# The down projection of a SwiGLU block: 16 of 22 inner tiles as a 2x2 block product with seven half products

## The chip, the cores and the metric

The kernel runs on one core of a Trainium2 chip. The core has five engines that work side by side, each through its own queue in order: TensorE (PE, matrix products; its weight loads are listed as PEld), VectorE (DVE), ScalarE (ACT), GpSimd (POOL) and SyncE (SP, which issues the transfers here). They meet at semaphores. Matrix products go to PSUM, eight banks of 128 x 512 float32; all else lies in SBUF. The metric is the device time of one execution in microseconds, the median of several.

## The reference

A trunk of two layers over 512 tokens with 1024 channels. Each layer is FFN, mixer, FFN, each between two RMS norms:

```python
def swiglu_ffn(h, w_gate, w_up, w_down):
    return (jax.nn.silu(h @ w_gate) * (h @ w_up)) @ w_down

def reference(x, ...):
    for l in range(DEPTH):
        h = rms_norm(x, norm_pre[l, 0])
        x = x + 0.5 * rms_norm(swiglu_ffn(h, ffn1_w_gate[l], ...), norm_post[l, 0])
        h = rms_norm(x, norm_pre[l, 1])
        x = x + rms_norm(hybrid_mixer(h, ...), norm_post[l, 1])
        h = rms_norm(x, norm_pre[l, 2])
        x = x + 0.5 * rms_norm(swiglu_ffn(h, ffn2_w_gate[l], ...), norm_post[l, 2])
    return x
```

The inner width of an FFN is 2816, which is 22 tiles of 128. So there are four FFNs, and in each a down projection: 512 tokens x 2816 by 2816 x 1024. The mixer (attention, convolution, gated linear attention) is not touched.

## The kernel before

**Precision.** Every float32 operand is split into a high part, which ScalarE casts to the type `float32r`, and a low part, which VectorE makes as operand minus high part (`split`, lines 107 and 108). A product is three matmuls: high by high, high by low, low by high. All matmuls are issued by `mm` (line 66).

**Gate and up.** `block_tiles` computes inner tiles 3 to 21 as 2x2 block products in seven half products each ("product" g; 12 matmuls of 256 columns). Weights are loaded raw, summed and split six products ahead of use; the split normalised input stands in `xh` and `xl` (128 x 8 x 512). Of every product ScalarE or VectorE takes results from PSUM (`cp`), and the tile's hidden values land in `hid[f]` (128 inner x 512 tokens), with f from 0 to 21. `between(g)` lets other work into that loop.

**Down.** `out_proj` has eight banks `o`: four token groups i of 128 times two column halves h of 512. For each inner tile k it loads 128 x 1024 weights (512 KB), splits them (`whi`, `wlo`) and the hidden tile (`sh`, `sl`), and issues 8 x 3 matmuls of 512 columns, hidden tile stationary and weights moving. The last four tiles (`TAIL`) go token group by token group, so that `finish(i)` (post norm, residual, next pre norm) of a finished group runs beside the matmuls of the next one. `early` loads the first weights of the next block.

**What sets the order.** A tile framework allocates buffers from pools in turn and puts in the waits; what passes through `pinned` or `mm` keeps the order in which it is written, other instructions can be moved ahead within their engine. Pool `wp` has five buffers for `whi`, five for `wlo`, and three for `raw`, each with room for two loads of 512 KB: a `raw` buffer is free when both its loads are used. Pool `tp` has slots of 128 x 512, 16 under tag "t", 14 under "s", 10 under "q". In the profile `whi<-raw` is the cast of weights and `wlo<-raw,whi` their low part, `sh<-hid` and `sl<-hid,sh` the same of a hidden tile.

## Time and profile before

| | |
|---|---|
| Median of 3 runs (lowest to highest) | 2366.95 us (2366.07 to 2367.29) |
| The profiled execution, its time and its span | 2367.24 us, 2365.5 us |
| TensorE busy | 2347.7 us, 99%, at the full clock |
| VectorE, ScalarE, GpSimd busy | 1629.1, 1117.9, 181.1 us |
| Down projections of the four FFNs, first `o` matmul at | 244.0, 1066.7, 1416.7, 2239.4 us |
| Transfers | 231.74 MB, mean 98 GB/s |

How to read it: a matmul's duration overlaps with the next one's, so what a matmul takes of TensorE is the distance from its start to the next start. The same holds, more weakly, on the other engines: an instruction's duration includes a tail under which the next one on the engine already begins; a consumer on another engine waits for the end. The busy share is an average over stages that differ widely.

### The profile page before, as it was taken

What the parts mean: (1) busy time and instruction counts of PE and PEld (TensorE: products, weight loads), DVE (VectorE), ACT (ScalarE), POOL (GpSimd) and SP (SyncE); (2) the same over time, 40 slices, a digit from 0 to 9 for tenths busy, and PEclk for the clock granted to TensorE, in tenths of its full rate; (3) what the DMA queues carried; (4) which work ended last, traced back from release to release, by engine and by line L of the source; (5) the groups of instructions that cost most, each with busy time, mean ns of one, the idle gap of its engine ahead of it and who ended that gap; (6) DMA issues with size and microseconds to landing.
All of it is one profiled execution on the core that took longest, in us unless ns stands there. A gap on an engine that the chain in (4) does not pass through costs nothing. (4 is left out here: it accounts for less than half of the span.)

```text
span 2365.5 us, 35797 instructions
## 1 busy us (share of the span) xinstructions
PE 2347.7 (99%) x14264; PEld 2094.3 (89%) x14264; DVE 1629.1 (69%) x2329; ACT 1117.9 (47%) x2148; POOL 181.1 (8%) x287
## 2 busy tenths in 40 slices
PE   8999999999999999999999999999999999999998
PEld 7999888887888899998899998888878888999987
DVE  7888436859965388884388883478599644888833
ACT  5556325644323365563356562356333333555622
POOL 0000001201011100000000000012010211000000
PEclk9999999999999999999999999999999999999999
DMA  5333323231333223333233343241313332333430
GB/s 171 96 102 107 142 89 103 69 94 54 108 90 107 81 72 108 108 110 141 71 87 102 100 133 116 73 116 55 110 54 106 91 95 75 90 108 108 134 107 36
DMA packets 307159, 231.74 MB, mean 98 GB/s; under 512 B 11722, under 2 KB 284140, under 8 KB 306992
## 3 DMA queue, kind: packets, MB, share of 16 engines
q1 hardware_dynamic: 306992, 229.46, 32.5%
q8 instruction: 111, 1.82, 0.3%
q14 instruction: 56, 0.46, 0.1%
HBM read 227.32 MB, written 2.10 MB: 97 GB/s over the span
## 5 line engine op out<-in xcount | busy, mean ns | idle before, releaser
L108 DVE TENSOR_TENSOR wlo<-raw,whi 128x1024 fp32r<-128x1024 f32 (+1 forms) x266 | 330.4, 1249 | 224.5 <-ACT whi L107 217.6
L107 ACT CAST whi<-raw 128x1024 fp32r<-128x1024 f32 (+1 forms) x266 | 278.1, 1046 | 399.3 <-PE gate L66 131.3
L336 DVE TENSOR_TENSOR wlo<-raw,whi 128x1024 fp32r<-128x1024 f32 (+1 forms) x304 | 331.1, 1089 | 125.0 <-ACT whi L334 124.8
L334 ACT CAST whi<-raw 128x512 fp32r<-128x512 f32 x532 | 315.1, 619 | 154.0 <-DVE raw L336 154.0
L66 PE MATMUL o<-whi,sh 128*128 128x512 f32 x704 | 274.2, 389 | 0.0
L66 PE MATMUL o<-wlo,sh 128*128 128x512 f32 x704 | 273.9, 389 | 0.0
L66 PE MATMUL o<-whi,sl 128*128 128x512 f32 x704 | 273.9, 389 | 0.0
L336 DVE TENSOR_TENSOR raw<-raw 128x512 f32<-128x512 f32 x304 | 209.3, 688 | 6.4
L108 DVE TENSOR_TENSOR sl<-hid,sh 128x512 fp32r<-128x512 f32 x88 | 60.0, 689 | 190.9 <-ACT sh L107 190.9
L66 PE MATMUL A<-xh,wlo 128*128 128x256 f32 x608 | 172.1, 283 | 0.0
L66 PE MATMUL A<-xl,whi 128*128 128x256 f32 x608 | 172.1, 283 | 0.0
L66 PE MATMUL A<-xh,whi 128*128 128x256 f32 x608 | 172.0, 283 | 0.0
L706 DVE SCALAR_TENSOR_TENSOR y<-u,cw,y 128x511 f32<-128x511 f32 (+14 forms) x240 | 166.7, 755 | 0.0
L107 ACT CAST sh<-hid 128x512 fp32r<-128x512 f32 x88 | 54.4, 622 | 230.5 <-PE o L66 230.5
L66 PEld LDWEIGHTS o<-whi,sl 128*128 128x128 f32 x704 | 132.1, 188 | 27.4
L66 PEld LDWEIGHTS o<-whi,sh 128*128 128x128 f32 x704 | 132.2, 188 | 27.3
L66 PEld LDWEIGHTS o<-wlo,sh 128*128 128x128 f32 x704 | 132.2, 188 | 27.2
L66 PE MATMUL gate<-xh,whi 128*128 128x512 f32 x384 | 151.3, 394 | 0.0
L66 PE MATMUL gate<-xh,wlo 128*128 128x512 f32 x384 | 149.8, 390 | 1.3 <-DVE wlo L108 1.3
L66 PE MATMUL gate<-xl,whi 128*128 128x512 f32 x384 | 149.6, 390 | 0.0
L195 POOL TENSOR_TENSOR rs<-ms,mhalf 128x1 f32<-128x1 f32 x48 | 30.9, 644 | 1454.4 <-DVE ms L193 1454.4
L66 PEld LDWEIGHTS A<-xh,whi 128*128 128x128 f32 x608 | 116.7, 192 | 0.2
(278 smaller groups left out, 6227.1 us busy)
## 6 DMA issues: line engine op xcount, KB each, us to landing
raw<-in_w_in_dram SPq DMA_DIRECT2D x108, 512.0 KB, 4.8
raw<-in_ffn_w_down_dram SPq DMA_DIRECT2D x88, 512.0 KB, 4.4
raw<-in_ffn_w_gate_dram SPq DMA_DIRECT2D x152, 256.0 KB, 3.3
raw<-in_ffn_w_up_dram SPq DMA_DIRECT2D x152, 256.0 KB, 4.6
raw<-in_w_branch_dram SPq DMA_DIRECT2D x24, 512.0 KB, 3.7
raw<-in_w_out_dram SPq DMA_DIRECT2D x16, 512.0 KB, 4.4
raw<-in_ffn_w_gate_dram SPq DMA_DIRECT2D x12, 512.0 KB, 4.8
raw<-in_ffn_w_up_dram SPq DMA_DIRECT2D x12, 512.0 KB, 4.6
```

The lines of the kernel that those rows point to most:

```text
L66: tc.keep_in_program_order(nc.tensor.matmul(*a, **k))
L107: nc.scalar.copy(hi, src)
L108: nc.vector.tensor_tensor(lo, src, hi.bitcast(F32), op=ALU.subtract)
L195: nc.gpsimd.tensor_tensor(rs, ms, mhalf[:, 0:1], op=ALU.pow)
L334: copy = lambda o, i: pin(nc.scalar.copy(o, i))
L336: tt = lambda o, a, b, op: pin(nc.vector.tensor_tensor(o, a, b, op=op))
L706: nc.vector.scalar_tensor_tensor(y[:, back:], u[:, :S - back], cw[:, c, j:j + 1], y[:, back:], op0=ALU.mult, op1=ALU.add)
```

## The change

For inner tiles 2 to 17 the down projection becomes a 2x2 block product. Tokens are halved (0 to 255 and 256 to 511), columns are halved (0 to 511, 512 to 1023), and the 16 inner tiles are halved (2 to 9, "near", and 10 to 17, "far"). Instead of eight block products there are seven, each 1024 inner x 256 tokens x 512 columns, on sums of weight blocks and of token blocks. Each is four steps, numbered 0 to 27 over all seven; a step covers two inner tiles of each half, loads a 256 x 512 block of weights (512 KB; S3 loads two), and issues 12 matmuls of 512 columns. In order:

- A11: near weights, first columns; no sum. Result copied out of bank pair A.
- S3: near minus far, second columns, into `kept`. Bank pair C, copied out.
- S2: `kept` minus near, first columns; first the near hidden tiles get the sum `S1` added. Bank pair A on top, copied to `u2`.
- A12: far weights, first columns; afterwards the far hidden tiles get the near ones added. Bank pair B.
- S1: minus `kept` minus far, second columns, with the token sum `S1`. Bank pair A on top, copied to `u4`.
- then inner tiles 0 and 1 in the classical way (24 matmuls each, all eight banks).
- S4: far weights, second columns. Bank pair A.
- A22: `kept` plus far, first columns. Bank pair C.

The last four tiles, 18 to 21, go as before through `out_proj`. The four copied results are combined with the banks in `results`, called by `finish`. `kept` uses the room of `xh`, two of the copies the room of `xl`; both are allocated anew for the next block (`room`). Token sums that need no down projection (`sum_tokens`) are made in the gate/up loop, two of 256 columns for each of the tiles 10 to 17. Three steps are prepared in the last products of gate/up, a fourth behind it; from then on step d+4 is prepared after product d has been issued.

```diff
+    def room(n, dt=F32R):
+        cur[n] = resid.tile([P, KC, S], dt, tag=n, name=n)
+        return cur[n]
...
+            if i == 0:
+                room("xh")
+                room("xl")
...
+        for k in range(nk - tail if fresh else 0):
...
+    class Down:
+        F0, NP = 2, 8
+        PER = NP // 2
+        ORDER = (("A11", ((0, 0),), "A"), ("S3", ((0, 1), (1, 1)), "C"), ("S2", ((0, 0),), "A"),
+                 ("A12", ((1, 0),), "B"), ("S1", ((1, 1),), "A"), ("S4", ((1, 1),), "A"), ("A22", ((1, 0),), "C"))
+        STEPS = 7 * PER
+        AHEAD = 4
+        MIDDLE, LAST = (0, 1), (18, 19, 20, 21)
...
+        def pairs(self):
+            self.s1 = [slot("S1", tag="q").rearrange("p (k t) -> p k t", k=2) for c in range(self.PER)]
+        def sum_tokens(self, f, n):
+            k = f - self.F0 - self.NP
+            if not 0 <= k < self.NP:
+                return
+            a, b = self.hid[k + self.F0], self.hid[f]
+            if n == 0:
+                pinned(nc.vector.tensor_tensor(self.s1[k // 2][:, k % 2], a[:, H1], b[:, H1], op=ALU.add))
+            else:
+                pinned(nc.vector.tensor_tensor(a[:, H1], a[:, H0], a[:, H1], op=ALU.add))
+        def prepare(self, d):
+            if d >= self.STEPS:
+                return
+            j, c = divmod(d, self.PER)
+            name, quads, _ = self.ORDER[j]
+            f0 = self.F0 + 2 * c
+            raws = []
+            for half, h in quads:
+                r0 = (f0 + half * self.NP) * P
+                raws.append(load_raw([(lambda r: r.rearrange("p (k c) -> p k c", k=2),
+                                       self.wd[r0:r0 + 2 * P, HS[h]].rearrange("(k p) c -> p k c", p=P))]))
+            kept = None if j == 0 else self.kept[:, 2 * c:2 * c + 2, :].rearrange("p k c -> p (k c)")
+            tt = lambda o, a, b, op: pinned(nc.vector.tensor_tensor(o, a, b, op=op))
+            src = raws[0]
+            if name == "S3":
+                tt(kept, raws[0], raws[1], ALU.subtract)
+                src = kept
+            if name == "S2":
+                tt(kept, kept, raws[0], ALU.subtract)
+                src = kept
+            if name == "S1":
+                pinned(nc.vector.scalar_tensor_tensor(src, kept, -1.0, raws[0], op0=ALU.mult, op1=ALU.subtract))
+            if name == "A22":
+                tt(src, kept, raws[0], ALU.add)
+            a = [self.hid[f0 + q] for q in range(2)]
+            b = [self.hid[f0 + self.NP + q] for q in range(2)]
+            if name == "S2":
+                for q in range(2):
+                    tt(a[q][:, H0], self.s1[c][:, q], a[q][:, H0], ALU.add)
+            part = {"A11": [x[:, H0] for x in a], "S3": [x[:, H1] for x in a], "S2": [x[:, H0] for x in a],
+                    "A12": [x[:, H0] for x in b], "S4": [x[:, H0] for x in b], "A22": [x[:, H1] for x in b],
+                    "S1": None}[name]
+            sh, sl = (slot(x, F32R, "s").rearrange("p (k t) -> p k t", k=2) for x in ("dh", "dl"))
+            hi, lo = (wp.tile([P, 1024], F32R, tag=t, name=t) for t in ("whi", "wlo"))
+            if part is None:
+                pinned(nc.scalar.copy(sh, self.s1[c]))
+            else:
+                for q in range(2):
+                    pinned(nc.scalar.copy(sh[:, q], part[q]))
+            pinned(nc.scalar.copy(hi, src))
+            if part is None:
+                tt(sl, self.s1[c], sh.bitcast(F32), ALU.subtract)
+            else:
+                for q in range(2):
+                    tt(sl[:, q], part[q], sh[:, q].bitcast(F32), ALU.subtract)
+            tt(lo, src, hi.bitcast(F32), ALU.subtract)
+            if name == "A12":
+                for q in range(2):
+                    tt(b[q][:, H0], b[q][:, H0], a[q][:, H0], ALU.add)
+            self.ready[d] = sh, sl, hi, lo
...
+        def product(self, d):
+            j, c = divmod(d, self.PER)
+            name, _, b = self.ORDER[j]
+            sh, sl, hi, lo = self.ready.pop(d)
+            for q in range(2):
+                w = slice(q * 512, (q + 1) * 512)
+                for i in range(2):
+                    mm_out(self.banks[b][i], slice(i * P, (i + 1) * P), sh[:, q], sl[:, q], hi[:, w], lo[:, w],
+                           st=(q == 0 and c == 0 and j in (0, 1, 3)))
+        def classical(self, f, first):
+            wh, wl = load_rows(self.wd, f)
+            sh, sl = slot("sh", F32R, "s"), slot("sl", F32R, "s")
+            split(sh, sl, self.hid[f])
+            for i, h in ((2, 1), (3, 1), (2, 0), (3, 0), (0, 0), (1, 0), (0, 1), (1, 1)):
+                mm_out(self.out[i][h], slice(i * P, (i + 1) * P), sh, sl, wh[:, HS[h]], wl[:, HS[h]],
+                       st=(first and (i, h) in ((2, 1), (3, 1))))
+        def run(self):
+            a0, b0, a1, b1, c0, d0 = (bank(n) for n in ("oA", "oB", "oA", "oB", "oC", "oD"))
+            c1, d1 = (bank(n, "pa") for n in ("oC", "oD"))
+            self.banks = {"A": (a0, a1), "B": (b0, b1), "C": (c0, c1), "D": (d0, d1)}
+            self.out = [[b0, a0], [b1, a1], [c0, d0], [c1, d1]]
+            self.kept, taps = room("xh", F32), room("xl", F32)
+            self.p1 = [taps[:, i, :] for i in range(2)]
+            p7 = [taps[:, 2 + i, :] for i in range(2)]
+            copy = lambda o, i: pinned(nc.scalar.copy(o, i))
+            while self.next < self.AHEAD:
+                self.ahead()
+            for d in range(self.STEPS):
+                j, c = divmod(d, self.PER)
+                self.product(d)
+                self.ahead()
+                if c < self.PER - 1:
+                    continue
+                if j == 0:
+                    for i in range(2):
+                        copy(self.p1[i], self.banks["A"][i])
+                if j == 1:
+                    for i in range(2):
+                        copy(p7[i], self.banks["C"][i])
+                if j == 2:
+                    self.u2 = [slot("u2") for i in range(2)]
+                    for i in range(2):
+                        copy(self.u2[i], self.banks["A"][i])
+                if j == 4:
+                    self.u4 = [slot("u4") for i in range(2)]
+                    for i in range(2):
+                        copy(self.u4[i], self.banks["A"][i])
+                    for i in range(2):
+                        pinned(nc.vector.tensor_tensor(self.u4[i], p7[i], self.u4[i], op=ALU.subtract))
+                    for f in self.MIDDLE:
+                        self.classical(f, f == self.MIDDLE[0])
+            return self.out
+        def results(self, i, banks):
+            tt = nc.vector.tensor_tensor
+            if i < 2:
+                tt(self.p1[i], banks[0], self.p1[i], op=ALU.add)
+                return [self.p1[i], banks[1]]
+            tt(self.u2[i - 2], banks[0], self.u2[i - 2], op=ALU.subtract)
+            tt(self.u4[i - 2], banks[1], self.u4[i - 2], op=ALU.add)
+            return [self.u2[i - 2], self.u4[i - 2]]
...
+                down.pairs()
+            u, j = divmod(g, 7)
+            if j in (2, 4) and u > 0:
+                down.sum_tokens(fs[u - 1], j // 4)
+            if g in (n - 5, n - 3, n - 1):
+                down.ahead()
...
+            sh, sl = slot("sh", F32R), slot("sl", F32R)
+        banks = down.run()
+        return out_proj(wd, NF, stat, TAIL, lambda i, b: finish(i, down.results(i, b)), upcoming, early, banks)
```

The order of instructions on the engines follows; a row has the line (of the file in question), the operation, out<-in and the size. VectorE before, where the old down projection begins; after the last hidden tile (`hid<-cp,hid`) there is one `wlo` and one `sl` per inner tile:

```order
L336 TENSOR_TENSOR cp<-C,cp 128x256
L336 TENSOR_TENSOR cp<-cp 128x256
L108 TENSOR_TENSOR sl<-hid,sh 128x512
L108 TENSOR_TENSOR wlo<-raw,whi 128x1024
L336 TENSOR_TENSOR hid<-cp,hid 128x512
L108 TENSOR_TENSOR wlo<-raw,whi 128x1024
```

VectorE with the change, one step of S2 (`xh_3042` is `kept`, `S1_648` the token sum, `dh` and `dl` the split hidden tiles; behind a row the engines or transfers whose semaphore it waits for):

```order
L510 TENSOR_TENSOR xh_3042<-xh_3042,raw_3173 128x1024 [waits DMAHW3_49]
L510 TENSOR_TENSOR hid_595<-S1_648,hid_595 128x256
L510 TENSOR_TENSOR hid_629<-S1_648,hid_629 128x256
L510 TENSOR_TENSOR dl_3179<-hid_595,dh_3178 128x256 [waits Activation_49]
L510 TENSOR_TENSOR dl_3179<-hid_629,dh_3178 128x256 [waits Activation_49]
L510 TENSOR_TENSOR wlo_3181<-xh_3042,whi_3180 128x1024 [waits PE_49,Activation_49]
```

Where one `sl` and one `wlo` stood, there are now six instructions, and three of them wait for ScalarE.

VectorE with the change, from the last preparation of S4 to the first classical tile (`wlo_3568`, `sl_3572`, inner tile 0):

```order
L510 TENSOR_TENSOR wlo_3552<-raw_3524,whi_3551 128x1024 [waits DMAHW2_49,Activation_49]
L605 TENSOR_TENSOR u4_3559<-xl_3043,u4_3559 128x512 [waits Activation_49]
L605 TENSOR_TENSOR u4_3560<-xl_3043,u4_3560 128x512 [waits Activation_49]
L113 TENSOR_TENSOR wlo_3568<-raw_3565,whi_3567 128x1024 [waits DMAHW3_49,PE_49,Activation_49]
L113 TENSOR_TENSOR sl_3572<-hid_588,sh_3571 128x512 [waits Activation_49]
```

The classical tile's low parts stand behind the preparations of S4, whose products come after it on TensorE, and behind the two `u4` subtractions. In the old order a tile's `wlo` and `sl` stood behind those of the tile before it.

ScalarE with the change, at the same place (`whi_3567` and `whi_3600` are the weights of the two classical tiles, `whi_3649` those of A22's first step):

```order
L581 COPY u4_3559<-oA_3034 128x512 [waits PE_49]
L581 COPY u4_3560<-oA_3036 128x512 [waits PE_49]
L112 CAST whi_3567<-raw_3565 128x1024 [waits DMAHW3_49,DVE_49]
L112 CAST sh_3571<-hid_588 128x512
...
L112 CAST sh_3803<-hid_646 128x512 [waits DVE_49]
L112 CAST whi_3600<-raw_3565 128x1024 [waits DMAHW4_49,PE_49]
L538 CAST whi_3649<-raw_3644 128x1024 [waits DMAHW5_49,DVE_49,PE_49]
```

The copies to `u4` wait for S1's last product. `whi_3567`, `whi_3600` and `whi_3649` are allocated in one and the same buffer of the five, the other four holding S4's steps; the second and the third wait for the last matmul (PE) that reads the one before.

More of the change, by code (lines that the diff above doesn't have):

```diff
@@ L96 @@
         nc.vector.memset(indic[c * CHUNK:(c + 1) * CHUNK, c:c + 1], 1.0 / 16.0)
-    xh = resid.tile([P, KC, S], F32R, name="xh")
-    xl = resid.tile([P, KC, S], F32R, name="xl")
+    cur = {}
+    def room(n, dt=F32R):
+        cur[n] = resid.tile([P, KC, S], dt, tag=n, name=n)
+        return cur[n]
     x_sb = [resid.tile([P, D], F32, name=f"x{i}") for i in range(NT)]
@@ L138, in mm_cols @@
         for k in ks:
-            mm(ps, wh[:, k, :], xh[:, k, :], start=(k == 0), stop=False)
-            mm(ps, wh[:, k, :], xl[:, k, :], start=False, stop=False)
-            mm(ps, wl[:, k, :], xh[:, k, :], start=False, stop=(k == KC - 1))
+            mm(ps, wh[:, k, :], cur["xh"][:, k, :], start=(k == 0), stop=False)
+            mm(ps, wh[:, k, :], cur["xl"][:, k, :], start=False, stop=False)
+            mm(ps, wl[:, k, :], cur["xh"][:, k, :], start=False, stop=(k == KC - 1))
     def proj_cols(w2d, c0, name, tag="pb"):
@@ L173, in mm_tok @@
             wh, wl = w[k]
-            mm(o, xh[:, k, t], wh, start=(first and k == 0), stop=False, skip_group_check=True)
-            mm(o, xh[:, k, t], wl, start=False, stop=False, skip_group_check=True)
-            mm(o, xl[:, k, t], wh, start=False, stop=(k == KC - 1), skip_group_check=True)
+            mm(o, cur["xh"][:, k, t], wh, start=(first and k == 0), stop=False, skip_group_check=True)
+            mm(o, cur["xh"][:, k, t], wl, start=False, stop=False, skip_group_check=True)
+            mm(o, cur["xl"][:, k, t], wh, start=False, stop=(k == KC - 1), skip_group_check=True)
     def load_g(row):
@@ L235, in post_norm, with load_rows, mm_out, out_proj @@
             nc.vector.scalar_tensor_tensor(x, tn[h], rs, x, op0=ALU.mult, op1=ALU.add)
-    def out_proj(w2d, nk, stat, tail, finish, upcoming, early):
-        banks = [[bank(f"o{i}{h}", "pb" if i < 3 else "pa") for h in range(2)] for i in range(NT)]
-        def mms(i, h, k, sh, sl, wh, wl):
-            t = slice(i * P, (i + 1) * P)
-            st, en = (k == 0), (k == nk - 1)
-            mm(banks[i][h], sh[:, t], wh[:, HS[h]], start=st, stop=False)
-            mm(banks[i][h], sh[:, t], wl[:, HS[h]], start=False, stop=False)
-            mm(banks[i][h], sl[:, t], wh[:, HS[h]], start=False, stop=en)
-        ld = lambda k: load_w([(lambda r: r, w2d[k * P:(k + 1) * P, :])], 1024)
-        for k in range(nk - tail):
+    def load_rows(w2d, k):
+        return load_w([(lambda r: r, w2d[k * P:(k + 1) * P, :])], 1024)
+    def mm_out(o, t, sh, sl, wh, wl, st=False, en=False):
+        mm(o, sh[:, t], wh, start=st, stop=False, skip_group_check=True)
+        mm(o, sh[:, t], wl, start=False, stop=False, skip_group_check=True)
+        mm(o, sl[:, t], wh, start=False, stop=en, skip_group_check=True)
+    def out_proj(w2d, nk, stat, tail, finish, upcoming, early, banks=None):
+        ld = lambda k: load_rows(w2d, k)
+        fresh = banks is None
+        if fresh:
+            banks = [[bank(f"o{i}{h}", "pb" if i < 3 else "pa") for h in range(2)] for i in range(NT)]
+        def mms(i, h, k, sh, sl, wh, wl):
+            mm_out(banks[i][h], slice(i * P, (i + 1) * P), sh, sl, wh[:, HS[h]], wl[:, HS[h]],
+                   fresh and k == 0, k == nk - 1)
+        for k in range(nk - tail if fresh else 0):
             wh, wl = ld(k)
@@ L319, in form @@
                 k0, t0 = {"B11": (0, 0), "B21": (4, 0), "B22": (4, 256)}[n]
-                self.parts[n] = [(xh[:, k0 + k, t0:t0 + 256], xl[:, k0 + k, t0:t0 + 256]) for k in range(4)]
+                self.parts[n] = [(cur["xh"][:, k0 + k, t0:t0 + 256], cur["xl"][:, k0 + k, t0:t0 + 256]) for k in range(4)]
             return self.parts[n]
@@ L443, in block_tiles, with __init__, ahead @@
                 summed(g - 1)
+    class Down:
[6 more added lines that the diff above has]
+        MIDDLE, LAST = (0, 1), (18, 19, 20, 21)
+        def __init__(self, wd, hid):
+            self.wd, self.hid = wd, hid
+            self.ready = {}
+            self.s1 = None
+            self.next = 0
+        def pairs(self):
[59 more added lines that the diff above has]
+            self.ready[d] = sh, sl, hi, lo
+        def ahead(self):
+            self.prepare(self.next)
+            self.next += 1
+        def product(self, d):
[58 more added lines that the diff above has]
+            return [self.u2[i - 2], self.u4[i - 2]]
```

9 lines of the change are left out of this document (5 added, 4 removed).

## The prediction

> **What bounds the kernel now.** I read the page first, then the busy time by stretches, then single rows of TensorE, VectorE and ScalarE around the start of the first down projection.
>
> ```profile
> span 2365.5 us, 35797 instructions
> PE 2347.7 (99%) x14264; PEld 2094.3 (89%) x14264; DVE 1629.1 (69%) x2329; ACT 1117.9 (47%) x2148; POOL 181.1 (8%) x287
> ```
>
> TensorE leaves 17.8 us of the span idle. So a matmul less is worth its spacing, as long as TensorE stays fed. By stretches (window; length, then busy us and count of each engine, clock, DMA share, GB/s):
>
> ```profile
> 100.00:240.00 140.00, 140.00 (x1169) 140.00 (x1168) 118.17 (x168) 83.73 (x183) 0.00 (x0) 1.00 0.36 105
> 240.00:365.00 125.00, 125.00 (x573) 104.29 (x572) 53.88 (x70) 45.40 (x74) 5.79 (x8) 1.00 0.30 105
> 1060.00:1070.00 10.00, 10.00 (x73) 9.43 (x72) 10.00 (x14) 7.85 (x14) 0.00 (x0) 1.00 0.81 273
> 1187.00:1200.00 13.00, 12.82 (x108) 12.54 (x106) 12.35 (x20) 9.15 (x20) 2.23 (x3) 1.00 0.58 163
> ```
>
> The gate/up stretch (row 1) and the down projection (row 2) never stop TensorE. VectorE is 84% busy in gate/up, but only 43% in the down projection. That spare 57% is what the change spends.
>
> **TensorE's gain.** The last down projection alone, matmuls into `o`:
>
> ```profile
> L66 PE MATMUL o<-whi,sh x176: 389/389/396, 2239.4 to 2358.4; 128*128 128x512 f32 x176
> L66 PE MATMUL o<-whi,sl x176: 388/389/389, 2239.9 to 2358.9; 128*128 128x512 f32 x176
> ```
>
> 528 matmuls start from 2239.4 to 2358.9: 119.5/527 = 0.2268 us each. The change issues 28 steps of 12 and 6 classical tiles of 24, that is 480. It removes 48 x 0.2268 = 10.9 us per FFN, 43.5 us in four. Shape and operands of a matmul stay, so does the spacing. A step takes TensorE 12 x 0.2268 = 2.72 us.
>
> **VectorE's price.** These rows of the old kernel hold every size needed (start, duration; back to back):
>
> ```profile
> 234.08 1.22 DVE L336 TENSOR_TENSOR wlo<-raw,whi 128x1024 fp32r<-128x1024 f32 x1
> 235.22 0.42 DVE L336 TENSOR_TENSOR cp<-C,cp 128x256 f32<-128x256 f32 x1
> 235.55 0.41 DVE L336 TENSOR_TENSOR cp<-cp 128x256 f32<-128x256 f32 x1
> 235.88 0.69 DVE L336 TENSOR_TENSOR wlo<-raw,whi 128x512 fp32r<-128x512 f32 x1
> 236.49 0.68 DVE L336 TENSOR_TENSOR hid<-cp,hid 128x512 f32<-128x512 f32 x1
> 237.09 2.35 DVE L108 TENSOR_TENSOR wlo<-raw,whi 128x1024 fp32r<-128x1024 f32 x2
> ```
>
> From start to start: 1024 columns 1.14, 512 0.60, 256 0.33; the result of a 1024 one is there after 1.22. ScalarE's casts:
>
> ```profile
> 234.39 0.61 ACT L334 CAST whi<-raw 128x512 fp32r<-128x512 f32 x1
> 234.90 1.05 ACT L107 CAST whi<-raw 128x1024 fp32r<-128x1024 f32 x1
> 235.85 0.37 ACT L334 COPY cp<-A 128x256 f32<-128x256 f32 x1
> 236.15 0.62 ACT L107 CAST sh<-hid 128x512 fp32r<-128x512 f32 x1
> ```
>
> 1024 columns 1.05 (0.95 start to start), 512 0.62 (0.51), 256 0.37 (0.3).
>
> Now the chain of a step whose weights are a sum: VectorE sums, ScalarE casts the sum to `whi`, VectorE subtracts to `wlo`. VectorE works in order, so it stands still while the cast runs, but for the two `dl`. The old gate/up has the same chain and the same standstill:
>
> ```profile
> 183.99 0.61 ACT L334 CAST whi<-raw 128x512 fp32r<-128x512 f32 x1
> 184.63 1.23 DVE L336 TENSOR_TENSOR wlo<-raw,whi 128x1024 fp32r<-128x1024 f32 x1 [0.26 <-ACT whi L334]
> DVE wlo L336 <- ACT whi L334: 124.8, 188, 1.5
> ```
>
> The cast ends at 184.60 and `wlo` starts at 184.63, a hand-over of 0.03. VectorE's time per step:
> - A11 and S4, no sum: two `dl` 0.66 + `wlo` 1.14 = 1.80.
> - S3, S1, A22: sum 1.22, hand-over, cast 1.05, hand-over, `wlo` 1.14 = 3.49 (the `dl`, 0.66, lie under the cast). S1's fused form is taken as a plain sum.
> - S2: sum 1.14, two token sums 0.66; ScalarE can cast tokens only after these (first sum done at 1.56, the casts from 1.59 and 1.92), then the weights from 2.19 to 3.24; `wlo` from 3.27, next step at 4.41.
> - A12: `dl` 0.66, `wlo` 1.14, two token sums 0.66 = 2.46.
>
> ScalarE needs some 1.6 per step (two token casts 0.6, weights 0.95) and sets no pace outside this chain. TensorE needs 2.72 per step: VectorE is slower in 16 of 28 steps. It starts with a lead. Steps 0 to 3 are made around the end of gate/up; the last `wlo` waits behind the last hidden tile (two Silu, product 0.60, two token casts, weight cast 1.05, `wlo`) and ends some 3.6 us after TensorE enters the down projection. From there VectorE's stream to the first classical tile is 4 x 3.49 + 4 x 4.41 + 4 x 2.46 + 4 x 3.49 + 4 x 1.80 = 62.6 us: S3, S2, A12, S1, and S4 as well. By the order of instructions S4's four preparations and two subtractions for `u4` (1.2) come **before** the classical tile's `wlo` (1.23), while TensorE executes the classical tile **before** S4. So that `wlo` is there at 3.6 + 62.6 + 1.2 + 1.2 = 68.6, and the tile's first matmul, which needs `whi` alone, can precede it: TensorE enters the classical tile effectively at 68.4. Its own 20 steps take 54.4. **Waits: 14.0 us** per FFN, some 7 within S2 and S1 (the first where a step of S2 takes 4.41 against 2.72) and 7 ahead of the classical tile.
>
> The second classical tile takes the `whi` buffer of the first (the other four hold S4). Its cast starts when the first tile's last matmul ends: 0.16 tail of the matmul + 0.04 + 1.05 + 0.03 + 1.22, less one matmul of 0.23 that needs `whi` alone: **2.3 us**. A22's first cast waits for the second tile in turn, and VectorE's queue behind it; but S4, ready since long, covers it: TensorE leaves the second tile at 81.6 and needs A22 from 92.5 on, one step each 2.72; VectorE has it at 84.1, 87.6, 91.1, 94.6. Zero. Without that cover it would be 2.5 more. The last four tiles' casts wait for S4 and A22 steps to leave their buffers; the last `wlo` comes at 103.1, needed after 103.4. Zero.
>
> Sum for an FFN: 14.0 + 2.3 - 10.9 = **+5.4 us**, four times +21.7.
>
> Bounds of the 14.0. Below: were there no standstill at hand-overs, S3, S1 and A22 would cost 2.94 and S2 3.60, the stream 54.9, and the wait 6.4: -2.2 per FFN. Under even that, with VectorE never late, the classical tile still waits for two `u4` copies, its casts, and `wlo` after product 19: 0.2 + 0.51 + 0.51 + 1.05 + 0.03 + 1.22 + ..., about 4: -4.6 per FFN. Above: loads. A step of S3 takes two loads of 512 KB, into a buffer that the step three before it frees; two such megabytes start at 3.7 and 4.9 and are needed at 10.6 and 14.1. The 273 GB/s of row 1060 moves 1 MB in 3.8: just in time; I take 0, and 2 us per FFN as the upper end. 38 loads instead of 22 over some 125 us are 159 GB/s.
>
> **Smaller terms.** In gate/up, eight tiles of an FFN get two token sums of 256, 0.66 us more per tile. A tile takes some 10.1 us, 16% of which, 1.6, VectorE stands idle: hidden, zero; if VectorE were the bound, 8 x 0.66 = 5.3 per FFN. The combining sums in `results` add 0.60 or 1.2 per token group on VectorE. For groups 0 to 2 later groups' matmuls cover them. At the very end the second Square must wait for a sum:
>
> ```profile
> 2359.42 0.60 ACT L191 ACTIVATE junk<-o 128x512 bf16<-128x512 f32 x1
> ```
>
> It starts 0.13 after its last matmul's end; behind two sums it starts about 0.65 later: +0.65. Where an FFN follows an FFN (row 1187: VectorE 12.35 of 13, TensorE idle 0.18) the 1.2 us of the last group go onto the path: +1.2, with 0 to 1.2 at the two starts of a mixer, taken as 0. The released `xh` and `xl` cost nothing: the next writer of `xl` comes some 6 us after group 1's last read.
>
> **Sum.** The profiled execution took 2367.24 us, 0.3 above the median of 2366.95. 2367.2 + 21.7 + 0.65 + 1.2 = 2390.8: **2391 us**.
>
> **Rivals.**
> 1. *TensorE's clock falls in the new waits.* After the waiting start of the program the same 256-column matmul is spaced 0.21 at first and 0.12 later:
>
> ```profile
> 13.06 0.41 PE L66 MATMUL pf<-whi,xh 128*128 128x256 f32 x1
> 13.27 0.41 PE L66 MATMUL pf<-wlo,xh 128*128 128x256 f32 x1
> 18.93 0.28 PE L66 MATMUL pf<-wlo,xh 128*128 128x256 f32 x1
> 19.05 0.28 PE L66 MATMUL pf<-whi,xl 128*128 128x256 f32 x1
> ```
>
> From 13.06 to 18.7, 27 matmuls lose 0.094 each: 2.5 us. Once per FFN, after the 7 us ahead of the classical tile, this gives +10: 2401. Against it: no row of this trace shows a fall from the full clock, since after that start TensorE hardly idles at all. Its idle time before 12.68 is
>
> ```profile
> 7.69 1.97 PE L71 MATMUL pt<-ident,hn 128*128 128x128 f32 x8 [7.69 <-DVE hn L210]
> 11.31 0.58 PE L66 MATMUL pf<-whi,xh 128*128 128x256 f32 x1 [1.65 <-ACT xh L107]
> 12.68 0.58 PE L66 MATMUL pf<-whi,xl 128*128 128x256 f32 x1 [0.58 <-DVE xl L108]
> ```
>
> 9.9 us, and behind its last matmul (2358.9 + 0.39) 6.2 of the 17.8. Chance 0.25. [...] The rows above agree with a slow start, and cannot show the fall.
>
> 2. *The hand-overs are hidden and VectorE is nearly in time* (the other side). Where the standstills cost nothing, 6.4 + 2.3 - 10.9 = -2.2 per FFN: 2367.2 - 8.8 + 1.9 = 2360. With VectorE never late, -4.6: 2351. It decides as soon as VectorE's stream to the classical tile stays below 57 us, where waits and saved matmuls balance. For it: VectorE has spare time over the whole down projection (71 of 125). Against it: 124.8 us of just this standstill in the rows. Chance 0.10.
>
> 3. *The saving in full*, 43.5 - 1.9: 2326. It needs both classical tiles prepared ahead. The single `whi` buffer that both share, free only when product 19 ends, excludes it. Chance 0.02.
>
> 4. *VectorE becomes the bound in gate/up also*, or loads come late: 2 to 5 more per FFN, 2399 to 2412. Against it the 1.6 us idle per tile. Chance 0.08.
>
> **How the numbers follow.** My forecast has 0.55 and its own range 2380 to 2398 (1 to 2 us per FFN for the start at 3.6 and the steps' rounding). The range 2364 to 2408 takes in rival 1 and most of rival 4 above, and reaches down toward rival 2. A difference under about 0.2%, 4.7 us, can't be told from none. Slower by more: 0.55 + 0.25 + 0.08 = 0.88, less 0.02 for mixtures near zero, 0.86; within: 0.05; faster: rivals 2 and 3 less what of them falls near zero, 0.09.
>
> **What would show it.** Right, if in the changed profile TensorE stands 1.5 to 2 us before each of S2's steps for `wlo`, some 7 us before the first matmuls into bank `oD`, and 2 to 2.5 before the second classical tile; if a down projection takes 124 to 128 us instead of 120.8; and if VectorE's longest new waits are `wlo` for ScalarE's `whi`. The clock rival shows as `o` matmuls of twice the spacing behind the 7 us. Wrong, if TensorE runs through S2 without a wait (the steps' cost), if the first tile's wait is about 4 us (VectorE in time), or if gate/up's stretches grow.

## The result, and the profile after

The changed kernel takes **2418.89 us** (median of four runs, 2416.68 to 2419.53), the kernel before on the same chip 2366.61 (2366.07 to 2367.29): a ratio of **1.0219**, 95% interval 1.0201 to 1.0237. It is slower by 52.3 us. The prediction was 2391, with a range of 2364 to 2408: the direction is right, and the loss was forecast too small, 24 us for 52.

The head of the changed kernel's page:

```profile
span 2417.8 us, 36165 instructions
PE 2339.3 (97%) x14072; PEld 2064.9 (85%) x14072; DVE 1855.4 (77%) x2745; ACT 1218.4 (50%) x2372; POOL 179.0 (7%) x287
```

TensorE issues 192 matmuls less (14264 before), yet its busy time falls by 8.4 us only, not by the 43.5 that 192 spacings are worth; its idle time grows from 17.8 to 78.5. VectorE has 226 us more to do.

The four down projections by stretches, the first and the last FFN's, of the kernel before and then of the changed one. Columns: window, length, then busy us and count of TensorE, its weight loads, VectorE, ScalarE and GpSimd, granted clock, DMA share, GB/s.

```profile
244.00:364.60 120.60, 120.60 (x539) 99.93 (x538) 49.48 (x62) 41.02 (x67) 5.79 (x8) 1.00 0.28 96
2239.40:2359.30 119.90, 119.89 (x530) 98.97 (x528) 44.07 (x53) 32.27 (x50) 1.65 (x3) 1.00 0.22 79
```

```profile
244.40:376.50 132.10, 118.28 (x491) 92.83 (x490) 99.93 (x146) 65.67 (x120) 5.35 (x7) 0.96 0.45 154
...
2280.20:2410.60 130.40, 116.69 (x482) 91.25 (x480) 96.26 (x141) 58.22 (x104) 1.65 (x3) 0.96 0.39 140
```

From the first `o` matmul to the end of the last one, a down projection takes 132.1, 131.7, 131.1 and 130.4 us, where it took 120.8, 120.8, 120.8 and 119.9: 43.1 of the 52.3 us. Two things are to be seen. TensorE idles 13.8 us of the first and 13.7 of the last; and the clock column says 0.96 where it said 1.00. Another 7.9 us lie just behind these stretches, as shown further below. The gate/up loops grew by 0.1 to 0.4 us each, and no wait of VectorE or ScalarE for a transfer is new.

Inside a stretch (the last FFN, TensorE's timeline: start, duration, operation; in brackets the idle time before it and who ended it), around the first classical tile:

```profile
2343.44 0.39 PE L66 MATMUL oA<-whi,dl 128*128 128x512 f32 x1
2348.45 0.80 PE L66 MATMUL oD<-whi,sh 128*128 128x512 f32 x1 [4.62 <-ACT sh L112]
2350.60 0.79 PE L66 MATMUL oD<-wlo,sh 128*128 128x512 f32 x1 [1.36 <-DVE wlo L113]
...
2351.80 0.63 PE L66 MATMUL oD<-whi,sh 128*128 128x512 f32 x1
2352.23 0.63 PE L66 MATMUL oD<-wlo,sh 128*128 128x512 f32 x1
...
2356.91 0.40 PE L66 MATMUL oB<-whi,sh 128*128 128x512 f32 x1
...
2358.76 0.39 PE L66 MATMUL oA<-whi,sl 128*128 128x512 f32 x1
2360.28 0.49 PE L66 MATMUL oD<-whi,sh 128*128 128x512 f32 x1 [1.13 <-ACT whi L112]
2361.54 0.50 PE L66 MATMUL oD<-wlo,sh 128*128 128x512 f32 x1 [0.77 <-DVE wlo L113]
```

From start to start TensorE stands 5.01 and 2.15 us ahead of the first classical tile, which is the predicted wait of 7. Behind it the same matmul of 512 columns is spaced 0.43 instead of 0.23, from 2351.80 until 2356.91; then the old spacing is back. That is the clock rival: the granted clock, third column from the end of the next row, stands at half from within the wait until then.

```profile
2346.60:2356.90 10.30, 7.09 (x15) 5.04 (x16) 8.76 (x14) 4.58 (x9) 0.00 (x0) 0.50 0.52 191
```

The second classical tile's wait of 1.52 and 1.26 follows: less two spacings of 0.23 that is 2.3, as predicted. In the first two FFNs, not in the last two, the clock falls once more behind this second wait (at half from 325.9 to 329.4 in the first). So there are six falls in four down projections.

VectorE in a step of S2, and ScalarE where S2 ends and A12 begins (timelines of the same FFN):

```profile
2301.42 1.23 DVE L510 TENSOR_TENSOR wlo<-xh,whi 128x1024 fp32r<-128x1024 f32 x1 [0.53 <-ACT whi L538]
2302.56 1.22 DVE L510 TENSOR_TENSOR xh<-xh,raw 128x1024 f32<-128x1024 f32 x1
2303.69 0.75 DVE L510 TENSOR_TENSOR hid<-S,hid 128x256 f32<-128x256 f32 x2
2304.58 0.76 DVE L510 TENSOR_TENSOR dl<-hid,dh 128x256 fp32r<-128x256 f32 x2
2305.87 1.23 DVE L510 TENSOR_TENSOR wlo<-xh,whi 128x1024 fp32r<-128x1024 f32 x1 [0.52 <-ACT whi L538]
```

```profile
2313.70 1.04 ACT L538 CAST whi<-xh 128x1024 fp32r<-128x1024 f32 x1
2314.65 1.07 ACT L581 COPY xl<-oC 128x512 f32<-128x512 f32 x2
2315.60 0.72 ACT L537 CAST dh<-hid 128x256 fp32r<-128x256 f32 x2
2316.22 1.06 ACT L538 CAST whi<-raw 128x1024 fp32r<-128x1024 f32 x1
```

A step is 4.45 us (2301.42 to 2305.87), forecast 4.41: sum, token sums, a stop, `dl`, a stop of 0.5 for the cast, `wlo`. The second fence shows a thing that the forecast left out: the two copies of S3's result to `xl` stand in ScalarE's queue between S2's last cast and A12's first one, and hold that up by 0.95.

### The profile page after: what moved, and what is told of

The parts are those of the page before. It is cut to its first block, busy times and chain, and to the rows that moved or that the text cites. A ratio compares the mean times of both kernels' runs of the same rounds, so it can differ in the third digit from the quotient of the medians.

```text
span 2417.8 us, 36165 instructions
## 1 busy us (share of the span) xinstructions
PE 2339.3 (97%) x14072; PEld 2064.9 (85%) x14072; DVE 1855.4 (77%) x2745; ACT 1218.4 (50%) x2372; POOL 179.0 (7%) x287
## 5 line engine op out<-in xcount | busy, mean ns | idle before, releaser
L352 DVE TENSOR_TENSOR wlo<-raw,whi 128x1024 fp32r<-128x1024 f32 (+1 forms) x304 | 331.1, 1089 | 108.8 <-ACT whi L350 108.0
L113 DVE TENSOR_TENSOR wlo<-raw,whi 128x1024 fp32r<-128x1024 f32 (+1 forms) x202 | 252.4, 1257 | 200.5 <-ACT whi L112 193.7
L112 ACT CAST whi<-raw 128x1024 fp32r<-128x1024 f32 (+1 forms) x202 | 210.6, 1045 | 387.2 <-PE gate L66 131.3
L510 DVE TENSOR_TENSOR wlo<-raw,whi 128x1024 fp32r<-128x1024 f32 x80 | 97.8, 1222 | 50.1 <-ACT whi L538 50.1
L538 ACT CAST whi<-raw 128x1024 fp32r<-128x1024 f32 x80 | 84.1, 1051 | 93.3 <-PE oA L66 38.1
L66 PE MATMUL oA<-wlo,dh 128*128 128x512 f32 x256 | 103.5, 404 | 18.5 <-DVE wlo L510 18.5
L350 ACT COPY cp<-A 128x256 f32<-128x256 f32 x228 | 84.5, 370 | 70.6 <-PE A L66 69.7
L66 PEld LDWEIGHTS A<-xl,whi 128*128 128x128 f32 x608 | 116.6, 192 | 0.2
L66 PEld LDWEIGHTS A<-xh,wlo 128*128 128x128 f32 x608 | 116.6, 192 | 0.0
L66 PE MATMUL oA<-whi,dh 128*128 128x512 f32 x256 | 101.3, 396 | 4.8 <-ACT whi L538 4.8
L66 PE MATMUL oA<-whi,dl 128*128 128x512 f32 x256 | 100.0, 390 | 0.0
```

The costliest lines, as they stand in the source:

```text
L66: tc.keep_in_program_order(nc.tensor.matmul(*a, **k))
L112: nc.scalar.copy(hi, src)
L113: nc.vector.tensor_tensor(lo, src, hi.bitcast(F32), op=ALU.subtract)
L350: copy = lambda o, i: pin(nc.scalar.copy(o, i))
L352: tt = lambda o, a, b, op: pin(nc.vector.tensor_tensor(o, a, b, op=op))
L510: tt = lambda o, a, b, op: pinned(nc.vector.tensor_tensor(o, a, b, op=op))
```

## The experiments

Each run was compared with the kernel before on the same chip; that kernel takes 2366.3 to 2366.9 on each chip that was used. All times are medians; the sum of the four down stages and the clock (mean granted share of TensorE's full clock) are those of the profiled execution.

| Run | us | ratio, 95% interval | four down stages, sum us | clock |
|---|---|---|---|---|
| before | 2366.6 | | 482.2 | 1.000 |
| after | 2418.9 | 1.0219 (1.0201 to 1.0237) | 525.2 | 0.991 |
| e1, clock kept at the first wait | 2410.4 | 1.0186 (1.0171 to 1.0201) | 518.1 | 0.998 |
| e2, classical tiles in their place | 2369.8 | 1.0012 (1.0003 to 1.0022) | 475.4 | 0.999 |
| e3, sums ahead | 2394.1 | 1.0116 (1.0099 to 1.0133) | 500.6 | 0.992 |
| e4, e2 and e3 | **2345.3** | **0.9910** (0.9895 to 0.9925) | 451.7 | 0.999 |
| e5, no combining sums | 2409.0 | 1.0182 (1.0166 to 1.0197) | 524.1 | 0.991 |
| e6, e4 with token sums on GpSimd | 2345.6 | 0.9911 (0.9895 to 0.9928) | 452.9 | 0.999 |
| e7, clock kept at both waits | 2416.4 | 1.0210 (1.0195 to 1.0225) | 522.4 | 1.000 |
| e8, the same with half the filling | 2409.0 | 1.0178 (1.0161 to 1.0195) | 515.7 | 0.999 |
| e9, the first wait half filled | 2419.0 | 1.0221 (1.0206 to 1.0236) | 524.9 | 0.994 |

**e1: what does the clock cost?** TensorE is kept busy ahead of the first classical tile with matmuls that nobody reads:

```diff
+                    for _ in range(30):
+                        mm(self.out[2][1][:, :P], ident, ident, start=True, stop=True, skip_group_check=True)
                     for f in self.MIDDLE:
                         self.classical(f, f == self.MIDDLE[0])
```

> The changed kernel with 30 needless matmuls of 128 columns (each some 0.21 us) ahead of the first classical tile, into a bank that this tile overwrites: TensorE is kept at work through the 7 us wait, and nothing waits less. Theory 1 (VectorE's late preparations make the waits, and the wait ahead of the classical tile makes the clock fall on top): the classical tiles' matmuls are spaced 0.23 instead of 0.43, which is worth 3 to 4 us in each FFN, 12 to 16 in all: about 2405 us. Rival A (the clock fall comes of something else, such as the load on the core, or the slow spacing is not the clock): no change, 2419. Rival B (the clock is the main loss of the change): 2385 or less.

Measured: 2410.4, 8.5 less than the changed kernel, where 12 to 16 was expected. Behind the first classical tile no matmul is spaced 0.43 any more. But in the second and third FFN the clock fell behind the *second* tile's wait; TensorE's timeline in the second:

```profile
1156.60 0.49 PE L66 MATMUL oD<-whi,sh 128*128 128x512 f32 x1 [1.13 <-ACT whi L112]
1157.86 0.50 PE L66 MATMUL oD<-wlo,sh 128*128 128x512 f32 x1 [0.77 <-DVE wlo L113]
...
1158.90 0.63 PE L66 MATMUL oD<-whi,sl 128*128 128x512 f32 x1
1159.33 0.63 PE L66 MATMUL oC<-whi,sh 128*128 128x512 f32 x1
```

In the first and the fourth FFN of this run the same wait, 1.52 and 1.26, is followed by matmuls at 0.23. So the clock costs something, and this run does not show all of it: these two falls are still in it.

**e7 and e8: the clock kept at both waits.** The same with further matmuls, on zeros, between the two classical tiles; they add nothing to the bank that they write. e8 differs from e7 in one number, 10 for 20.

```diff
+    zeros = const.tile([P, 64], F32, name="zeros")
+    nc.gpsimd.memset(zeros, 0.0)
...
-                    for f in self.MIDDLE:
+                    for f, n in zip(self.MIDDLE, (30, 20)):
+                        first = f == self.MIDDLE[0]
+                        for _ in range(n):
+                            mm(self.out[2][1][:, :P if first else 64], ident, ident if first else zeros, start=first,
+                               stop=True, skip_group_check=True)
```

> The changed kernel with TensorE kept busy through both waits: 30 matmuls of 128x128 ahead of the first classical tile (as in the run with a kept clock, 2410.4) and 20 more of 64 columns, on zeros, between the two classical tiles. Theory: what that run left of slow matmuls follows the second tile's wait of 1.5 and 1.3 us, which comes just after the first; with it covered no o matmul stands at 0.43 any more, and all four down stages come down to about 127.7 us (the shortest of that run's 128.9, 131.3, 130.2, 127.7): 2410.4 - 7 = 2403 us. Rival: those longer stages come from the waits themselves and the clock has nothing to do with them; then the time stays at 2410, or rises with the added matmuls.

Measured: 2416.4. The clock stayed at 1.000, and no `o` matmul is spaced 0.43, but the time did not come down: the filling was too long. Its rows in e7, then in e8 (x40 and x20: two records for each matmul):

```profile
2353.03 4.57 PE L66 MATMUL oD<-zeros,ident 128*128 128x64 f32 x40
```

```profile
2349.33 2.34 PE L66 MATMUL oD<-zeros,ident 128*128 128x64 f32 x20
...
2351.89 0.50 PE L66 MATMUL oD<-wlo,sh 128*128 128x512 f32 x1
```

I had taken the 64-column matmuls to be shorter than the 128-column ones; both take 0.23.

> As the run before it with TensorE kept busy through both waits (2416.4, no slow matmul left), but with 10 matmuls of 64 columns between the two classical tiles instead of 20. In that run the 20 took 4.57 us in the trace, 0.23 each, where the wait they were to fill is 2.8, so they held up the second tile themselves. Theory: 10 take 2.3, lie within the wait, and the full clock is kept: the down stages fall from 129.7 to 131.2 by some 2 us each, 2416.4 - 8 = 2408 us, and 11 below the changed kernel, which is what the two falls of the clock cost. Rival: the falls cost nothing beside the waits; then the time stays at 2416 to 2419.

Measured: 2409.0, with the filling inside the wait and the second tile at the place that it has without any (78.7 us into the last stage, as in e1). So the clock costs **9.9 us** in the changed kernel (2418.9 less 2409.0), or by the traces 9.5 over the four stages: 2.4 per FFN. Without it a down stage takes 129.6, 129.8, 128.6 and 127.7 us, still 7.9 to 9.0 more than before. The clock is a fifth of the loss, not its cause.

**e9: what makes the clock fall?** The first wait only half filled, 12 matmuls instead of e1's 30.

> The changed kernel with 12 instead of 30 matmuls of 128x128 ahead of the first classical tile (0.23 each: 2.7 us of the 5.0 us wait). TensorE then stands for two gaps of some 2.2 us with one matmul between. Theory one (a single gap of nearly 5 us makes the clock fall): the spacing behind the first tile's wait stays at 0.23, and the time is that of the 30, 2410 us. Theory two (what counts is the share of idle time over several us): the clock falls as in the changed kernel, 13 or more o matmuls at 0.43 behind the wait, and the time stays at 2417 to 2419 us.

Measured: 2419.0, as the changed kernel. TensorE's timeline:

```profile
2343.34 2.84 PE L66 MATMUL oD<-ident 128*128 128x128 f32 x24
2348.10 0.49 PE L66 MATMUL oD<-whi,sh 128*128 128x512 f32 x1 [1.92 <-ACT sh L112]
2350.25 0.80 PE L66 MATMUL oD<-wlo,sh 128*128 128x512 f32 x1 [1.66 <-DVE wlo L113]
...
2351.87 0.63 PE L66 MATMUL oD<-wlo,sh 128*128 128x512 f32 x1
```

Two gaps of 2.2 and 2.15 with one matmul between were enough: the matmuls behind them are spaced 0.43. That is the last FFN; the clock of the whole run, 0.994 against e1's 0.998, says that it was not there alone. The second theory's forecast came true, and the first one's did not: the clock fell without a single gap of 5. Two gaps of 0.79 and 1.26 (all gaps here from start to start) in each of S2's steps of 4.45 did not lower it; it stands at 1.00 through S2 of the changed kernel. The last section has more of these rows.

**e2: the classical tiles prepared in their place.** Their loads, casts and low parts take the place in VectorE's and ScalarE's queues that they have on TensorE, behind step 19 and ahead of S4, four items ahead of use like all others; so the `u4` subtractions no longer stand before them, and both tiles have buffers of their own.

```diff
+            self.items = [*range(20), *(("c", f) for f in self.MIDDLE), *range(20, self.STEPS)]
...
-            wh, wl = load_rows(self.wd, f)
-            sh, sl = slot("sh", F32R, "s"), slot("sl", F32R, "s")
-            split(sh, sl, self.hid[f])
+            sh, sl, wh, wl = self.ready.pop(("c", f))
...
+                        self.ahead()
```

> The changed kernel with the two classical tiles prepared in their place of the sequence, four items ahead, like the steps; the matmuls and their order stay. Theory 1: the 7 us ahead of the first classical tile and 2.3 ahead of the second go, and with them the fall of the clock (3 to 4); the waits within S2 and S1, some 7, stay. Per FFN 12 to 13 less, 50 in all: about 2368 us, no gain and no loss against the kernel before. Rival B (clock alone): 2405. Rival C (VectorE's total work in the down projection is the bound, wherever it stands): no change, 2419, the wait only moves to later steps.

Measured: 2369.8, 49.1 less. By the traces the four down stages lose 49.8 of their 525.2. TensorE enters both tiles without a wait, and the clock column of the four stages is back at 1.00. What S2 and S1 wait is unchanged. This one misplacement is nearly the whole loss: per FFN 6.7 ahead of the first tile (5.01 and 2.15 less two spacings), 2.3 ahead of the second, 2.4 of clock. These are 45.6 of the 49.8; the rest was not split up.

**e3: the weight sums ahead of the low parts.** Only the order on VectorE changes: a step's sums are issued before the low parts of the step before it, so that its cast runs under those.

```diff
             pinned(nc.scalar.copy(hi, src))
+            if d + 1 < self.STEPS and self.kept is not None:
+                self.sums(d + 1)
             if part is None:
                 tt(sl, self.s1[c], sh.bitcast(F32), ALU.subtract)
```

> The changed kernel with a step's sums issued ahead of the low parts of the step before, so that ScalarE's cast of the sum runs under VectorE's other work; every instruction stays, only VectorE's order differs. The classical tiles are left as in the change. Theory 1: the standstill at hand-overs goes (0.6 in each step of S3 and S1, 0.9 in one of S2), VectorE's stream to the classical tile shortens by 7 to 8 us per FFN, TensorE runs through S2 and S1 almost without a wait, but still waits some 7 ahead of the classical tile, with the clock falling: 2419 - 30 = 2389 us. Rival C (VectorE's work itself, not the hand-overs): 2 us per FFN at most, 2410 or more. Rival D (late loads): no change.

Measured: 2394.1, 24.8 less. VectorE's timeline in S2 of the last FFN now:

```profile
2279.41 1.22 DVE L505 TENSOR_TENSOR wlo<-xh,whi 128x1024 fp32r<-128x1024 f32 x1
2280.54 0.76 DVE L541 TENSOR_TENSOR hid<-S,hid 128x256 f32<-128x256 f32 x2
2281.21 1.22 DVE L541 TENSOR_TENSOR xh<-xh,raw 128x1024 f32<-128x1024 f32 x1
2282.35 0.76 DVE L505 TENSOR_TENSOR dl<-hid,dh 128x256 fp32r<-128x256 f32 x2
2283.02 1.22 DVE L505 TENSOR_TENSOR wlo<-xh,whi 128x1024 fp32r<-128x1024 f32 x1
```

3.61 us per step instead of 4.45 and no idle time. The prediction's lower bound of a step of S2, 3.60, is what the step costs once the standstill is gone. S1 has no wait left. The first classical tile's `wlo` is there 6.1 earlier (64.3 us into the stage instead of 70.4), which in four FFNs is nearly all of the 24.8; the two gaps ahead of that tile are still 3.04 and 3.99, and the clock still falls behind them.

**e4: both.** 

> Both edits of the last two runs: sums a step ahead, classical tiles prepared in their place. Theory 1: no waits of a length that counts in the down projection, no fall of the clock; the 48 matmuls saved show as 10 to 11 us per FFN, less 2 at the start of each following block (VectorE's combining sums) and 1 at the end: 2367 - 43 + 9 = 2333 us, up to 2342 with short waits left in S2. Rival C: 2390 or more. Rival D (late loads once VectorE runs faster): 2345 to 2380, with waits for transfers.

Measured: **2345.3**, less than either kernel, 0.9910 of the kernel before, and 3 above the upper end of what was expected. The two gains add: 49.1 + 24.8 = 73.9, measured 73.6. The last FFN's stage in its trace:

```profile
2225.50:2337.00 111.50, 109.80 (x481) 89.63 (x480) 94.47 (x141) 58.72 (x104) 1.65 (x3) 1.00 0.46 162
```

Of the 10.9 us that 48 matmuls less are worth, a down projection now keeps 6.2 to 8.3. What is left are three or four waits of some 1 us (from start to start) in S2, where VectorE takes 3.61 for TensorE's 2.72, and S3's sums, which now wait for their loads:

```profile
L542 DVE TENSOR_TENSOR xh<-raw 128x1024 f32<-128x1024 f32 x16 | 19.5, 1222 | 8.9 <-DMA raw<-in_ffn_w_down_dram 8.9
```

This is their group (busy us, mean ns, idle us before them): 8.9 us over the four FFNs. In the changed kernel VectorE came too late to wait for them.

**e5: the block starts.** The changed kernel with the banks handed to the norms as they are; the four copied results are left out.

```diff
         def results(self, i, banks):
-            tt = nc.vector.tensor_tensor
...
-            return [self.u2[i - 2], self.u4[i - 2]]
+            return banks
```

> The changed kernel without the combining sums behind the down projection: the banks go to the norms as they are, and the four copied results are not added (so the output lacks these parts of four of the seven products). Everything else stays, the copies too. Theory: the block starts behind a down projection are late because VectorE does these sums ahead of the next block's low parts: the two mixer starts lose 2.4 us each, the start of an FFN behind an FFN 1.9, the end 1.0, in all 7.7; so 2418.9 - 7.7 = 2411 us, while the down stages keep their 130.4 to 132.1. Rival: the starts are late because the last tiles' own casts and the next block's first casts queue behind the preparations of A22; then the time stays at 2417 to 2419.

Measured: 2409.0, 9.9 less, where 7.7 was expected. In the traces the span is 10.7 shorter; the down stages lose 1.1 of it, and 1.3 lie ahead of the first one, which begins at 243.1 instead of 244.4 and before which nothing was edited. The offset of the changed kernel to the kernel before grows by 2.4 us in the first 8 us of either mixer and by 2.1 at the FFN behind an FFN, and the end is 1.0 later: without the sums the growth at the starts is gone. ScalarE's longest wait of the changed kernel in the first mixer's start (engine, line, whom it waits for; us, times, longest), and VectorE's rows there:

```profile
ACT junk L196 <- DVE u L616: 2.3, 1, 2.3
```

```profile
382.46 0.68 DVE L616 TENSOR_TENSOR u<-oC,u 128x512 f32<-128x512 f32 x1
383.07 0.68 DVE L617 TENSOR_TENSOR u<-oD,u 128x512 f32<-128x512 f32 x1
383.66 1.28 DVE L239 SCALAR_TENSOR_TENSOR tn<-u,g 128x512 f32<-128x512 f32 x2
384.86 0.68 DVE L113 TENSOR_TENSOR xl<-pt,xh 128x512 fp32r<-128x512 f32 x1
```

The two sums of the last group (1.2 us) stand ahead of the norm and of the next block's `xl`. The cost is more than that 1.2, since ScalarE's Square waits for the sum and the chain of the norm starts later.

**e6: the token sums on GpSimd.** From e4, the 16 sums of 256 columns that S2 and A12 need per FFN, moved from VectorE to GpSimd.

```diff
-                    tt(a[q][:, H0], self.s1[c][:, q], a[q][:, H0], ALU.add)
+                    pinned(nc.gpsimd.tensor_tensor(a[q][:, H0], self.s1[c][:, q], a[q][:, H0], op=ALU.add))
...
-                    tt(b[q][:, H0], b[q][:, H0], a[q][:, H0], ALU.add)
+                    pinned(nc.gpsimd.tensor_tensor(b[q][:, H0], b[q][:, H0], a[q][:, H0], op=ALU.add))
```

> The kernel of the run with both changes of order (2345.3), with the 16 token sums of 256 columns of S2 and A12 on GpSimd, which is idle there, instead of VectorE. Theory: the waits of some 1 us per step that are left in S2 come from VectorE's time per step; each step of S2 loses 0.66 us of it, and of A12 too. The down stages of 111.6 to 114.6 us then come near to 480 x 0.2268 = 108.9: some 3 us less in each of four, 2345.3 - 12 = 2333 us. Rival: GpSimd's sums come late, as its old rows of 128x512 take 1.5 us each, and ScalarE's token casts then wait for them, or they slow VectorE's rows of 1024 columns; then 2345 or above.

Measured: 2345.6, no change; the rival holds. GpSimd's, VectorE's and ScalarE's timelines in the last FFN of e6 (two of S2's sums, then A12's first and the next three):

```profile
2228.41 2.53 POOL L548 TENSOR_TENSOR hid<-S,hid 128x256 f32<-128x256 f32 x2 [2.63 <-DVE dl L506]
...
2255.28 9.61 POOL L528 TENSOR_TENSOR hid<-hid 128x256 f32<-128x256 f32 x1 [24.33 <-DVE dl L506]
2264.85 2.13 POOL L528 TENSOR_TENSOR hid<-hid 128x256 f32<-128x256 f32 x3
```

```profile
2228.59 1.76 DVE L506 TENSOR_TENSOR wlo<-raw,whi 128x1024 fp32r<-128x1024 f32 x1
2230.27 1.75 DVE L542 TENSOR_TENSOR xh<-raw 128x1024 f32<-128x1024 f32 x1
...
2263.08 1.22 DVE L556 SCALAR_TENSOR_TENSOR raw<-xh,raw 128x1024 f32<-128x1024 f32 x1
```

```profile
2264.92 1.29 ACT L606 COPY u<-oA 128x512 f32<-128x512 f32 x2 [5.35 <-POOL hid L528]
```

S2 itself gains: a step takes VectorE 2.94 instead of 3.61, and over the four FFNs TensorE's waits in S2 come to 7.9 us less than in e4. The gain is lost elsewhere: 7.3 ahead of S1's first step and 1.7 in S3. Where both engines work at once, the rows of one of them are longer in this run. Beside S2's sums, which GpSimd makes around the end of gate/up, VectorE's rows of 1024 columns take 1.75 instead of 1.22. Beside A12, VectorE works row upon row until 2264.30 at its old 1.22, and GpSimd's first sum stands for 9.61 us; the three behind it, while VectorE stands still, take 0.71 each. A12's 32 sums of the four FFNs take 69.4 us, four times the 17.35 of these eight. ScalarE's copies to `u2` wait 5.35 for that sum, and behind them TensorE stands 1.8 us ahead of S1's first step. The first sum, from 2255.28 to 2264.89, lasts past a dozen VectorE instructions and ends 0.59 behind the last of them; why was not shown.

## Why the prediction was right and wrong, point by point

It forecast 2390.8; 28.1 us more were measured, which is past its range. Three steps failed: the clock's fall was left out of the sum, the wait of 14.0 was too small, and the mixer starts were taken as 0. By the runs these are 9.5 for the clock, 11.8 within the down stages at full clock (e8), 6.1 for block starts and the end, and 0.7 spread over the rest. A down projection takes 130.4 to 132.1, outside the 124 to 128 that the prediction gave as a sign of being right.

- **Direction and mechanism: right.** VectorE is too slow in S3, S2 and S1 since it stands still for ScalarE's cast. The row of the changed kernel is `DVE wlo L510 <- ACT whi L538`, 66.2 us in 71 waits. Of these some 27 are the standstills in S3, S2 and S1, 0.5 to 0.9 each; 30.0 are four waits of 6.7 to 8.3 for A22's first cast, which hold up nothing, as TensorE enters A22 without a wait. And VectorE's order puts the first classical tile behind S4. e3 and e2 remove the one and the other, and with both (e4) 73.6 us come back of the 95.8 between the changed kernel and the full saving (52.3 lost and 43.5 planned). Of the other 22, some 13 are waits left in S3 and S2, and 7.9 the block starts, which e4's trace has unchanged.
- **Saving of 10.9 per FFN: right**, as a saving of TensorE's work. At full clock the matmuls of a stage still are spaced 0.227.
- **VectorE's step times: nearly right.** S2 4.45 for 4.41; S1 3.61 for 3.49.
- **The 14.0 us: mis-sized.** In the last FFN the first classical tile's `wlo` is used 70.4 us into the stage, not at 68.6. The waits within S2 and S1 come to 9.0 for 7, the wait ahead of the tile to 6.7 for 7. The 1.8 are 0.5 up to S2's first step, 0.1 in S2, 0.8 in A12 and S1's first step, 0.4 in S1. The 0.8 has its cause in the ScalarE rows 2314.65 to 2316.22: S3's copies, which no term of the sum had. Another 0.5 is the wider spacing (0.34 to 0.56) of the first matmuls behind each of the two waits. With the forecast 5.4 this is nearly all of the 7.9 that the stage takes more at full clock (e8). In e8's first two FFNs about one us more comes on top, in waits of S3, S2 and S1; its cause was not followed up.
- **2.3 for the second classical tile, zero for A22, for the last four tiles' casts, for gate/up and for the loads: right**, by the rows shown and by the waits that are not there. That the load term was zero only because VectorE was late shows in e4.
- **The clock: the step that failed as a choice.** Rival 1 was given 0.25, as no row of the trace before was seen to show a fall. That trace does hold one, in the idle time behind the last matmul, which ends at 2359.3; these rows have the clock at 1.00, then at 0.50:

```profile
2359.30:2363.20 3.90, 0.00 (x0) 0.00 (x0) 2.92 (x5) 0.78 (x3) 0.55 (x1) 1.00 0.13 47
2363.40:2365.40 2.00, 0.00 (x0) 0.00 (x0) 0.00 (x0) 0.00 (x0) 0.00 (x0) 0.50 0.35 130
```

So that trace has a fall behind 4.0 us of idle time, and a wait of 7 was forecast. The price was right, 2.5 per FFN and +10 in all against 9.9 measured, but in part by luck: it had one fall per FFN, and there are two shorter ones in each of the first two. (The 27 matmuls of its sum are 21 and eight transposes in the trace, with a loss of 2.4 in place of 2.5.) The changed kernel has the fall behind a gap of 5.01 and one of 2.15: 0.43 instead of 0.23. As e9 shows, a single gap of 5 is not needed.
- **Mixer starts taken as 0, bounded by 1.2: wrong.** Measured 2.4 each, 2.1 at the FFN behind an FFN (forecast 1.2), 1.0 at the end (0.65): 7.9 for 1.85. The bound counted the two sums alone, and not that the norm's Square, and with it the chain to the next block, waits for them.
- **The range** took in the clock rival or late loads above the forecast, but not the clock together with two terms that were each too small; they are not alternatives, and they added.
- **Rival 2** (hand-overs hidden, 2351 to 2360) did not occur by itself. e3 builds its condition and gives 2394, since a tile prepared too late stays late: the rival's sum puts that tile's `wlo` at some 61 us into the stage (3.6, 54.9 and 2.4), e3 has it at 64.3, and the clock, which the rival left out, falls in the gaps ahead of it. **Rival 3** called the saving excluded by the buffer that both tiles share. That held for this order; e2 frees it by preparing both ahead.

## What to carry to other kernels

When work moves from the bound engine to one with spare time, lay out that engine's queue in order and time it up to each consumer, copies on the third engine included: VectorE had 57% spare here, and the loss came from two instructions queued in an order other than TensorE's, and from a standstill for a cast in each step. Both were mended by order alone, and 52 us lost became 21 won. Price a wait that comes to several us on TensorE with the clock's fall behind it (here 2.4 us per FFN, for waits of 5.01 and 2.15), and add it to the forecast rather than beside it; that the clock falls at all could be read here in the trace before, 4.0 us behind the last matmul's end.

## What the runs showed of the hardware that was not expected

- The clock fell for idle time that comes in pieces: 2.2 and 2.15 us with one matmul between (e9, last FFN), and in some FFNs 1.52 and 1.26 (the changed kernel's first and second, e1's second and third; not in the other FFNs of these two runs, with the same wait). It did not fall for 0.79 and 1.26 in every 4.45 of S2 (the changed kernel).
- What decides between equal waits was not shown. TensorE was busy, as the profile counts it, for 0.00, 1.52, 0.00, 1.51, 1.11 and 0.61 us of the 3.41 ahead of the changed kernel's six falls. In e1 the second FFN's wait lies within the first of these rows, 1.51 us busy, and the clock falls behind it; the fourth FFN's equal wait is divided between the other two, 2.28 and 2.65 busy, and it does not:

```profile
1155.45:1158.86 3.41, 1.51 (x6) 1.05 (x6) 1.23 (x1) 1.04 (x1) 0.00 (x0) 1.00 0.02 5
...
2350.12:2353.53 3.41, 2.28 (x11) 1.54 (x9) 1.18 (x3) 1.09 (x2) 0.00 (x0) 1.00 0.00 0
2353.53:2356.95 3.42, 2.65 (x11) 1.99 (x11) 0.97 (x1) 0.00 (x0) 0.00 (x0) 1.00 0.30 80
```

- In the changed kernel the clock stood at half for 6.8, 6.8, 10.2 and 10.2 us at the first wait of the four FFNs, and for 3.4 behind the second waits of the first two FFNs. It was back 3.8 to 6.3 us after the first tile's second matmul; in the last FFN that is 14 matmuls of 512 columns, 2350.60 to 2356.91.
- A float32 matmul of 128 x 128 by 64 columns took as long as one by 128, 0.23 us: 20 take 4.57 in e7 and 10 take 2.34 in e8, and of 128 columns 12 take 2.84 in e9.
- VectorE's operations of 1024 columns took 1.75 instead of 1.22 us beside S2's GpSimd sums (e6). GpSimd's sums of 256 columns took 0.71 while VectorE stood still, and A12's first one took 9.61 beside VectorE working without a pause.
